# The norms' weights loaded with the first block of x, the first loads in order of use, and three constants made later

## The chip, the cores and the metric

The kernel runs on one core of a Trainium2 chip. The metric is the device time of one execution in microseconds (us). The core has TensorE (PE in the profile) for matmuls, VectorE (DVE), ScalarE (ACT) and GpSimd (POOL) for elementwise work, and SyncE (SP), which here only issues DMAs. SP, ScalarE and GpSimd each have a DMA queue of their own.

## The reference

The reference computes one step of a two-layer encoder for 256 prompt tokens and 32 sample tokens (288 columns), model width 1024, all in float32. Cut to what matters here:

```python
def rmsnorm(x, g):
    y = x * rsqrt(mean(x * x, axis=-1, keepdims=True) + 1e-6)
    return y * g

# layer 0 (layer 1 has another attention in the first two lines)
qa, ka, va, qb, kb, vb = proj_ab(rmsnorm(x, g_mix[0]), w_in_ab)
x = x + merge_heads(chunk_band_attn(qa, ka, va, rel_bias), stick_break_attn(qb, kb, vb)) @ w_out_ab
x = x + memory_attn(rmsnorm(x, g_xattn[0]), mem_k, mem_v)
x = x + swiglu(rmsnorm(x, g_ffn[0]))
# behind layer 1
y = rmsnorm(x, g_final)
```

There are nine norm weights g of 1024 numbers each (two layers of mix, xattn, mem and ffn, and the final one).

## The kernel before

Activations lie transposed: 8 blocks of 128 features by 288 tokens, block k in `x[k]`. Two blocks share a tile (`xh`, four tiles; L72, L73). The norm weights lie in a tile `gain` of 128 x 72 numbers, one column for each of the 9 norms and 8 blocks (L71).

Each weight matrix comes in units of 128 x 1024 floats: 8 blocks of 128 x 128, one for each block of features. float32 accuracy is had from three matmuls of a shorter type: a unit is split into a rounded part `hi` (a cast on ScalarE, L156) and the rest `lo` (a subtraction on VectorE, L157), the scaled activations likewise into `hh` (ScalarE, L291) and `hl` (VectorE, L294), and `mm3` (L183) issues hi x hh, hi x hl and lo x hh. The norm's row factor is applied after the projection; its sum of squares comes from `sq` (ScalarE, L243) and `ssq` (VectorE or GpSimd, L251), summed over features by the matmuls `nrm`.

**The start.** 32 small matmuls of an identity with itself (L134, `warm`) come first on TensorE; their sum is 32 times an identity. Then the first three projections (query, key and value of the first head pair) are computed side by side (`side_by_side`, L816): for each block k of x the three units' blocks, nine matmuls, 72 in all, and behind them the norm's sums `nrm`. The three units stand in a layout of their own, `w_first`: the 24 blocks in the order in which the matmuls use them, eight to a tile (`first`, three tiles), so block k of x uses blocks 3k to 3k+2. The casts of these tiles are cut into seven pieces (L1018): columns 0 to 384, 384 to 768 and 768 to 1024 of the first tile, halves of the other two. The loop at L1019 writes them between the splits of x's blocks.

**The loads** at the start (L84 to L92): on SP's queue the first 384 columns of the first weight tile, x's first tile (blocks 0 and 1), the gains, the rest of the first weight tile, the second weight tile, x's third tile and the third weight tile; on ScalarE's queue x's second and fourth tile. Behind them on SP come the units of the next projections (`st`, four buffers, shared with `first`).

**Constants.** `more_constants` (L140) is called at L1027, behind the loop. It makes on VectorE `ident` (the sum of the warming matmuls divided by 32), `fold` and `fold4` (sums of pieces of it) and `ntrir` (a copy of a triangular mask in the short type). `ident` is used first by the matmuls `nr` that spread the norm's row factor, and by all transposes; `fold` first by the sample tokens' attention, `fold4` by the gates of layer 1, `ntrir` by the stick-breaking heads.

**The order** on each engine is not the order of the code: a scheduler places the instructions, with the dependences that the code adds (`not_before`, L167). `behind` (L164) holds instructions of the first norm that the weight splits of the first heads must not pass.

**The first softmax** (`attend_prompt`, L406, and `softmax`, L386): scores `sc`; on VectorE the bias and maximum (L397); on ScalarE the exponentials `e` (L399); on VectorE reciprocals (L400) and the scaling of e (L402); on TensorE the transposes `tp` (L422 to L424); on ScalarE their copies `pt` (L428); on TensorE the products `po`.

Of the kernel before, what the change touches and what calls it, by code (L numbers as in the profile page):

```python
# [8 lines left out]
F32 = mybir.dt.float32  # L9
# [3 lines left out]
AF = mybir.ActivationFunctionType  # L13
ALU = mybir.AluOpType

P = 128
NT = 288
NP = 256
NS = 32
KT = 8  # L20
# [6 lines left out]
def encoder_step(ctx: ExitStack, tc: tile.TileContext, a):  # L27
# [6 lines left out]
    cst = ctx.enter_context(tc.tile_pool(name="cst", bufs=1))  # L34
    wp = ctx.enter_context(tc.tile_pool(name="wp", bufs=4))
    big = ctx.enter_context(tc.tile_pool(name="big", bufs=1))
# [5 lines left out]
    V, S, G, T, DMA = nc.vector, nc.scalar, nc.gpsimd, nc.tensor, nc.sync  # L42
# [25 lines left out]
        return T.matmul(out, lhsT, rhs, start=start, stop=stop, skip_group_check=True)  # L68


    gain = cst.tile([P, 9 * KT], F32, name="gain")  # L71
    xh = [big.tile([P, 2 * NT], F32, tag=f"x{i}", name=f"x{i}") for i in range(4)]  # L72
    x = [xh[k // 2][:, (k % 2) * NT:(k % 2) * NT + NT] for k in range(KT)]  # L73


    first = [wp.tile([P, 1024], F32, tag="st", bufs=4, name=f"first{i}") for i in range(3)]
# [1 line left out]
    def first_part(i, c0, c1):  # L78
        DMA.dma_start(first[i][:, c0:c1], a["w_first"][i][:, c0:c1])

    def x_part(i, eng=DMA):
        eng.dma_start(xh[i], a["xT"][:, 2 * i * NT:2 * (i + 1) * NT])

    first_part(0, 0, 384)  # L84
    x_part(0)
    x_part(1, S)
    x_part(3, S)
    DMA.dma_start(gain, a["gains"])
    first_part(0, 384, 1024)
    first_part(1, 0, 1024)  # L90
    x_part(2)
    first_part(2, 0, 1024)  # L92


    mean1 = cst.tile([P, 2], F32, name="mean1")
# [9 lines left out]
    ntri = cst.tile([P, P], F32, name="ntri")  # L105
    G.memset(ntri, -1.0)
    G.affine_select(out=ntri, in_=ntri, pattern=[[-1, P]], compare_op=ALU.is_ge, fill=0.0, base=0, channel_multiplier=1)
    ntrir = cst.tile([P, P], F32R, name="ntrir")
# [23 lines left out]
    warm = ps.tile([P, 512], F32, tag="at", bufs=4, name="warm")  # L132
    for i in range(32):
        warmed = T.matmul(warm[:, 0:P], identb, identb, start=i == 0, stop=i == 31)  # L134
    ident = cst.tile([P, P], F32, name="ident")
    fold = cst.tile([P, 2, 32], F32, name="fold")

    fold4 = cst.tile([P, 16], F32, name="fold4")

    def more_constants():  # L140
        V.tensor_scalar(ident, warm[:, 0:P], 1.0 / 32.0, None, op0=ALU.mult)
        by_head = ident.rearrange("p (j i q) -> p j i q", j=2, i=2)
        V.tensor_tensor(fold, by_head[:, :, 0], by_head[:, :, 1], ALU.add)
        V.tensor_tensor(fold4, fold[:, 0, 0:16], fold[:, 1, 0:16], ALU.add)
        V.tensor_copy(ntrir, ntri)

    wtab = cst.tile([P, 2], F32, name="wtab")
    S.activation(wtab, mean1, AF.Exp)
# [15 lines left out]
    began, behind, loads = [], [], []  # L164
# [620 lines left out]
    def evac_kv(cur, p, dst):  # L785
        t = tok("kv")

        def go():
            i = V.tensor_tensor(t, p[:, :NT], cur.r, ALU.mult)
            store(dst, t)  # L790
            return i

        cur.then(go)
        return t

    def rel_prompt(h):

        t = tok("bi")
        G.memset(t[64:128, 192:256], NEG)
        for p, n in ((0, 256), (64, 192)):  # L800
            G.dma_start(t[p:p + 64, 0:n], bass.AP(tensor=lined.tensor, offset=lined.offset + 384 * h + p + 1, ap=[[1, 64], [1, n]]))
        return t
# [6 lines left out]
    def mix_ab(cur, nxt, memory, w0):  # L809
        o = ([tok("oh", F32R) for _ in range(KT)], [tok("ol", F32R) for _ in range(KT)])  # L810
        qs, ks, vs, vns = {}, {}, {}, {}
        w = a["w_ab"]

        biases = {}

        def side_by_side():  # L816
            p = [att("pj"), acc("pj"), acc("pj")]
            with tc.issue_after(warmed.ins):
                for k in range(KT):
                    for u in range(3):  # L820
                        b = 3 * k + u
                        i = mm3(p[u][:, :NT], w0[b // 8], b % 8, cur.h, k, k == 0, k == KT - 1)
                        if k in (0, 5, 7) and u == 2:
                            began.append(i.ins)
            cur.y = cur.norm.columns()
            tick()
            return p

        def proj(j):
            hurry[0] = j < 4  # L830
            b = 12 * (j // 4) + j % 4
            kv = 8 * (j // 4) + j % 4
            p = side_by_side() if j == 0 else (project(w[b + 4 * i], cur.h) for i in range(3))
            p = iter(p)
            qs[j] = evac_q(cur, next(p), j < 4)
            ks[j] = evac_kv(cur, next(p), a["kv0"][kv])
            if j < 4:
                biases[j] = [rel_prompt(2 * j + i) for i in range(2)]
            vs[j] = evac_kv(cur, next(p), a["kv0"][kv + 4])

        def attention(j):
            args = (qs[j], ks[j], vs[j], vns, j)
            if j < 4:
                return attend_prompt(*args, biases.pop(j), o[0][j], o[1][j], (128, 0), True)
            return stick_prompt(*args, o[0][j], o[1][j])

        def attend(j):
            return later(attention(j), j == 0)

        def sample(g):  # L850
            two = (2 * g, 2 * g + 1)
            ck, cv = cached(g, lambda i: (a["cab"][2 * i], a["cab"][2 * i + 1]), 1 if g == 0 else 6)
            args = ([qs[j] for j in two], [ks[j] for j in two], two, vns, ck, cv)
            oo = ([o[0][j] for j in two], [o[1][j] for j in two])
            if g < 2:
                bias = rel_sample(g)
                yield 1
                yield from attend_sample(*args, bias, oo, True)
            else:
                yield from stick_sample(*args, oo)  # L860

        active.append(cur.scale())
        pairs(proj, attend, sample, memory, (0, 0, 0, 0, 2, 2, 2, 8))
        out_project(a["w_oab"], o, nxt, [6, 7])

# [158 lines left out]
            cur.norm.add(x[m - 2], V)  # L1024
    cur.norm.add(x[KT - 2], V)
    cur.norm.add(x[KT - 1], V)
    more_constants()  # L1027
    memories = [Memory(0), Memory(1)]
    for layer in range(2):
        nxt = Next(2 + layer)  # L1030
# [44 lines left out]
def _pack(inputs):  # L1075

    import numpy as np

    g = {k: np.asarray(v) for k, v in inputs.items()}

    def units(w):
        n = w.shape[1] // 128
        return w.reshape(8, 128, n, 128).transpose(2, 1, 0, 3).reshape(n, 128, 1024)

    def feats(t):
        n = t.shape[0]
        return t.T.reshape(8, 128, n).transpose(1, 0, 2).reshape(128, 8 * n)

    def keysT(c):
        n = c.shape[1] // 8  # L1090
        return c.reshape(128, n, 4, 128).transpose(1, 3, 2, 0).reshape(n, 128, 512)

    def vals(c):
        return c.reshape(128, -1, 512).transpose(1, 0, 2)

    x = np.concatenate([g["x_prompt"][0], g["x_sample"][0]], axis=0)
    gains = np.stack([g["g_mix"][0], g["g_mix"][1], g["g_xattn"][0], g["g_xattn"][1], g["g_mem"][0], g["g_mem"][1],
                      g["g_ffn"][0], g["g_ffn"][1], g["g_final"]])
    w_ab = units(g["w_in_ab"][0])
    w_g = np.pad(g["w_in_c"][0][:, 3072:], ((0, 0), (0, 16)))  # L1100
    cab = [keysT(g["cache_a_k"][0, 0])[0], vals(g["cache_a_v"][0, 0])[0],
           keysT(g["cache_b_k"][0, 0])[0], vals(g["cache_b_v"][0, 0])[0]]
    out = {
        "xT": feats(x), "memT": feats(g["mem_prompt"][0]),
        "gains": gains.reshape(9, 8, 128).transpose(2, 0, 1).reshape(128, 72),
        "w_ab": w_ab, "w_first": w_ab[[0, 4, 8]].reshape(3, 128, 8, 128).transpose(1, 2, 0, 3).reshape(128, 3, 1024).transpose(1, 0, 2), "w_oab": units(g["w_out_ab"][0]),
        "w_c": units(g["w_in_c"][0][:, :3072]), "w_g": w_g.reshape(8, 128, 32).transpose(1, 0, 2).reshape(128, 256), "w_oc": units(g["w_out_c"][0]),
        "w_xq": np.stack([units(w) for w in g["w_xq"]]), "w_xk": np.stack([units(w) for w in g["w_xk"]]),
        "w_xo": np.stack([units(w) for w in g["w_xo"]]),
        "w_xv": g["w_xv"].reshape(2, 2, 4, 128, 4, 256).transpose(0, 4, 1, 3, 2, 5).reshape(2, 4, 2, 128, 1024),  # L1110
        "w_gate": np.stack([units(w) for w in g["w_gate"]]), "w_up": np.stack([units(w) for w in g["w_up"]]),
        "w_down": g["w_down"].reshape(2, 22, 128, 8, 128).transpose(0, 2, 3, 1, 4).reshape(2, 128, 22, 1024).transpose(0, 2, 1, 3),
        "cab": np.stack(cab), "cck": keysT(g["cache_c_k"][0, 0]), "ccv": vals(g["cache_c_v"][0, 0]),
        "cmk": g["cache_mem_k"][:, 0].reshape(2, 256, 4, 2, 128).transpose(0, 2, 4, 3, 1).reshape(2, 4, 128, 512),
        "cmv": g["cache_mem_v"][:, 0].reshape(2, 2, 128, 4, 256).transpose(0, 3, 2, 1, 4).reshape(2, 4, 128, 512),
        "clf": g["cache_c_logf"][0, 0], "rel": g["rel_bias_a"][0].T[:, ::-1], "b_f": g["b_f_c"][0].reshape(16, 1),
    }
    return {k: np.ascontiguousarray(v) for k, v in out.items()}
# [29 lines left out]
```

## Time and profile before

| | us |
|---|---|
| median of 3 runs | 961.99 (961.39 to 962.18) |
| the profiled execution | 961.8 |
| its span, first to last instruction | 960.1 |
| TensorE busy | 946.0 (99%) |
| VectorE busy | 592.5 (62%) |
| ScalarE busy | 484.3 (50%) |
| mean granted TensorE clock | 0.998 |

A row of the timeline has start and duration in us, the engine, the line of the kernel, the operation, the tiles written and read without their numbers, the shapes, the count, and in brackets how long the engine sat idle before it and what ended that. An engine's name with a q (SPq) is its instruction queue, where DMAs are issued. In the stretches each engine's busy time stands with its instruction count in brackets. Starts of a pipelined engine may lie closer together than a duration, so what an instruction costs in a row of others is read from start to start.

### The profile page before, as it was taken

The page shows a single profiled execution, that of the slowest core. Times are in us where ns is not written, and L with a number is a line of the kernel's source. Part 1 is how long each engine was busy: PE and PEld are TensorE (multiplying, and loading weights), DVE is VectorE, ACT ScalarE, POOL GpSimd, SP SyncE. Part 2 cuts the span into 40 slices and gives each one's busy share as a digit, 9 for nine tenths or more (in the row PEclk, how much of TensorE's full clock was granted, in tenths as well). Part 3 has the DMA queues.
Part 4 walks back from the last instruction along what each step waited for, and adds up shares of the span by engine and source line. Part 5 has one row for each costly group of instructions (what it writes and reads, how often), then busy time and mean ns, then how long its engine had stood idle before and what let it go on. Part 6 is the DMA issues. An engine that isn't in the chain of part 4 may idle for free.

```text
span 960.1 us, 19047 instructions
## 1 busy us (share of the span) xinstructions
PE 946.0 (99%) x7476; PEld 912.3 (95%) x7476; DVE 592.5 (62%) x1137; ACT 484.3 (50%) x860; POOL 239.3 (25%) x358
## 2 busy tenths in 40 slices
PE   8999999999999999999999999999999999999997
PEld 7889999999999999999999999999989999999996
DVE  6786556676765555855466666667658555555452
ACT  5566777544554444444346454455446544444331
POOL 4341123400222222410125432532012222222010
PEclk9999999999999999999999999999999999999999
DMA  7665446544344444454455454545425444444431
GB/s 274 195 211 198 156 167 184 189 154 130 120 158 160 171 172 158 175 199 175 168 207 188 165 201 165 182 153 189 158 79 176 155 174 162 169 167 163 175 111 50
DMA packets 49258, 160.97 MB, mean 168 GB/s; under 512 B 7304, under 2 KB 8136, under 8 KB 49168
## 3 DMA queue, kind: packets, MB, share of 16 engines
q1 hardware_dynamic: 44976, 149.12, 45.3%
q0 software_dynamic: 3904, 10.04, 3.0%
q8 instruction: 59, 0.97, 0.4%
q10 hardware_dynamic: 288, 0.59, 0.2%
q14 instruction: 31, 0.25, 0.1%
HBM read 149.58 MB, written 10.15 MB: 166 GB/s over the span
## 4 chain that ended last, share of the span: by engine, by line
PE 92%; DVE 3%; ACT 2%; DMA 1%; issue 1%; POOL 0%; DVEq 0%; SPq 0%; ACTq 0%; POOLq 0%
PE pj L68 52%; PE dn L68 15%; PE op L68 10%; PE mv L68 5%; PE po L68 1%; PE xo L68 1%; PE zb L68 1%; PE xs L68 1%; PE sc L68 1%; DVE lo L157 1%; DMA st<-w_ab 1%; ACT hi L156 1%; PE nrm L68 1%; ACT e L399 1%; PE xss L68 1%
## 5 line engine op out<-in xcount | busy, mean ns | idle before, releaser
L156 ACT CAST hi<-st 128x1024 fp32r<-128x1024 f32 x257 | 269.5, 1050 | 320.4 <-issue 128.0
L68 PE MATMUL pj<-hh,hi 128*128 128x288 f32 (+1 forms) x1344 | 399.8, 298 | 1.1 <-ACT hh L291 1.1
L68 PE MATMUL pj<-hh,lo 128*128 128x288 f32 (+1 forms) x1344 | 395.8, 294 | 0.0
L68 PE MATMUL pj<-hl,hi 128*128 128x288 f32 (+1 forms) x1344 | 394.2, 293 | 0.5 <-DVE hl L294 0.5
L157 DVE TENSOR_TENSOR lo<-st,hi 128x1024 fp32r<-128x1024 f32 x257 | 320.7, 1248 | 97.5 <-PE dn L68 42.7
L68 PEld LDWEIGHTS pj<-hh,hi 128*128 128x128 f32 x1344 | 253.0, 188 | 8.5 <-issue 5.7
L68 PEld LDWEIGHTS pj<-hl,hi 128*128 128x128 f32 x1344 | 253.1, 188 | 0.9 <-DVE hl L294 0.9
L68 PEld LDWEIGHTS pj<-hh,lo 128*128 128x128 f32 x1344 | 252.5, 188 | 0.2 <-DVE lo L157 0.2
L68 PE MATMUL dn<-fh,hi 128*128 128x288 f32 x400 | 108.8, 295 | 0.0
L68 PE MATMUL dn<-fh,lo 128*128 128x288 f32 x352 | 103.8, 295 | 0.0
L68 PE MATMUL dn<-fl,hi 128*128 128x288 f32 x304 | 89.5, 294 | 0.0
L68 PE MATMUL op<-ol,hi 128*128 128x288 f32 x256 | 75.7, 296 | 0.0
L68 PE MATMUL op<-oh,hi 128*128 128x288 f32 x256 | 75.7, 298 | 0.0
L68 PE MATMUL op<-oh,lo 128*128 128x288 f32 x256 | 75.3, 295 | 0.0
L68 PEld LDWEIGHTS dn<-fh,hi 128*128 128x128 f32 x400 | 72.6, 188 | 0.0
L68 PEld LDWEIGHTS dn<-fh,lo 128*128 128x128 f32 x352 | 66.2, 188 | 0.0
L251 POOL TENSOR_TENSOR ssq<-ssq,sq 128x288 f32<-128x288 f32 (+1 forms) x35 | 36.4, 1041 | 114.7 <-ACT sq L243 70.8
L754 POOL TENSOR_TENSOR fl<-us,fh 128x288 fp32r<-128x288 f32 x38 | 33.8, 890 | 120.0 <-ACT fh L753 120.0
L749 DVE TENSOR_TENSOR us<-pj,rstd 128x288 f32<-128x288 f32 x44 | 20.1, 458 | 60.8 <-PE pj L68 60.8
L750 POOL TENSOR_TENSOR gs<-gs,sg 128x288 f32<-128x288 f32 x44 | 38.8, 883 | 74.3 <-ACT sg L748 72.8
L68 PEld LDWEIGHTS dn<-fl,hi 128*128 128x128 f32 x304 | 57.2, 188 | 0.0
L68 PEld LDWEIGHTS op<-ol,hi 128*128 128x128 f32 x256 | 48.2, 188 | 0.6 <-issue 0.4
(268 smaller groups left out, 1260.8 us busy)
## 6 DMA issues: line engine op xcount, KB each, us to landing
st<-w_gate SPq DMA_DIRECT2D x44, 512.0 KB, 3.5
st<-w_up SPq DMA_DIRECT2D x44, 512.0 KB, 3.2
st<-w_down SPq DMA_DIRECT2D x44, 512.0 KB, 3.2
st<-w_c SPq DMA_DIRECT2D x24, 512.0 KB, 3.3
st<-w_ab SPq DMA_DIRECT2D x21, 512.0 KB, 4.7
st<-w_xk SPq DMA_DIRECT2D x16, 512.0 KB, 4.0
st<-w_xv SPq DMA_DIRECT2D x16, 512.0 KB, 3.5
st<-w_xq SPq DMA_DIRECT2D x16, 512.0 KB, 3.4
```

Of the source, the lines that this page charges most:

```text
L68: return T.matmul(out, lhsT, rhs, start=start, stop=stop, skip_group_check=True)
L156: a = S.copy(hi, st[:, c0:c1])
L157: b = V.tensor_tensor(lo, st[:, c0:c1], hi.bitcast(F32), ALU.subtract)
L251: eng.tensor_tensor(s[:, :self.n], self.acc[i][:, :self.n], q[:, :self.n], ALU.add)
L399: S.activation(out[:, c0:c1], out[:, c0:c1], AF.Exp, bias=mx, scale=-1.0, accum_out=sm)
L749: V.tensor_tensor(us, pu[:, :NT], cur.r, ALU.mult)
L750: G.tensor_tensor(gs, gs, sg, ALU.mult)
L754: G.tensor_tensor(lo, us, hi.bitcast(F32), ALU.subtract)
```

## The change

The gains are no longer a tensor of their own: they are laid in front of x in the input `xT`, and x's first tile becomes 72 columns wider to hold them. On ScalarE's queue the first load is now the gains with block 0, then x's second tile. On SP's queue: 384 columns of the first weight tile, block 1 by itself, the rest of the first weight tile, x's third tile, the second weight tile, half of the third, x's fourth tile, the other half. `ident` is made by ScalarE behind the loop; `fold`, `fold4` and `ntrir` are made by VectorE after the key projection of the third head pair in the code, not before the last instruction in `behind`.

```diff
-    gain = cst.tile([P, 9 * KT], F32, name="gain")
-    xh = [big.tile([P, 2 * NT], F32, tag=f"x{i}", name=f"x{i}") for i in range(4)]
-    x = [xh[k // 2][:, (k % 2) * NT:(k % 2) * NT + NT] for k in range(KT)]
+    G0 = 9 * KT
+    xh = [big.tile([P, 2 * NT + (0 if i else G0)], F32, tag=f"x{i}", name=f"x{i}") for i in range(4)]
+    gain = xh[0][:, 0:G0]
+    x = [xh[k // 2][:, (0 if k > 1 else G0) + (k % 2) * NT:][:, :NT] for k in range(KT)]
...
-    def x_part(i, eng=DMA):
-        eng.dma_start(xh[i], a["xT"][:, 2 * i * NT:2 * (i + 1) * NT])
-
+    def x_part(i):
+        DMA.dma_start(xh[i], a["xT"][:, G0 + 2 * i * NT:G0 + 2 * (i + 1) * NT])
+
+    S.dma_start(xh[0][:, 0:G0 + NT], a["xT"][:, 0:G0 + NT])
+    S.dma_start(xh[1], a["xT"][:, G0 + 2 * NT:G0 + 4 * NT])
     first_part(0, 0, 384)
-    x_part(0)
-    x_part(1, S)
-    x_part(3, S)
-    DMA.dma_start(gain, a["gains"])
+    DMA.dma_start(x[1], a["xT"][:, G0 + NT:G0 + 2 * NT])
     first_part(0, 384, 1024)
+    x_part(2)
     first_part(1, 0, 1024)
-    x_part(2)
-    first_part(2, 0, 1024)
+    first_part(2, 0, 512)
+    x_part(3)
+    first_part(2, 512, 1024)
...
     def more_constants():
-        V.tensor_scalar(ident, warm[:, 0:P], 1.0 / 32.0, None, op0=ALU.mult)
         by_head = ident.rearrange("p (j i q) -> p j i q", j=2, i=2)
-        V.tensor_tensor(fold, by_head[:, :, 0], by_head[:, :, 1], ALU.add)
-        V.tensor_tensor(fold4, fold[:, 0, 0:16], fold[:, 1, 0:16], ALU.add)
-        V.tensor_copy(ntrir, ntri)
+        for i in (V.tensor_tensor(fold, by_head[:, :, 0], by_head[:, :, 1], ALU.add),
+                  V.tensor_tensor(fold4, fold[:, 0, 0:16], fold[:, 1, 0:16], ALU.add),
+                  V.tensor_copy(ntrir, ntri)):
+            not_before(i, behind[-1])
...
             if j < 4:
                 biases[j] = [rel_prompt(2 * j + i) for i in range(2)]
+            if j == 2:
+                more_constants()
             vs[j] = evac_kv(cur, next(p), a["kv0"][kv + 4])
...
     cur.norm.add(x[KT - 1], V)
-    more_constants()
+    S.activation(ident, warm[:, 0:P], AF.Copy, scale=1.0 / 32.0)
```

The scheduler moves more than the code does. ScalarE at the start, from its first work on data to the second half of the second weight tile, before (`first_83` to `first_85` are the three weight tiles, `x_79` to `x_82` the four tiles of x):

```order
L156 CAST hi_177<-first_83 128x384
L291 ACTIVATE hh_183<-x_79,gain 128x288
L291 ACTIVATE hh_189<-x_79,gain 128x288
L156 CAST hi_177<-first_83 128x384
L291 ACTIVATE hh_195<-x_80,gain 128x288
L156 CAST hi_177<-first_83 128x256
L243 ACTIVATE sq_203<-x_79 128x288
L291 ACTIVATE hh_205<-x_80,gain 128x288
L156 CAST hi_179<-first_84 128x512
L243 ACTIVATE sq_209<-x_79 128x288
L156 CAST hi_179<-first_84 128x512
L291 ACTIVATE hh_213<-x_81,gain 128x288
```

And now (numbers one lower, `x_78` the first tile of x with the gains in it):

```order
L294 ACTIVATE hh_183<-x_78 128x288
L159 CAST hi_177<-first_82 128x384
L294 ACTIVATE hh_189<-x_78 128x288
L159 CAST hi_177<-first_82 128x384
L294 ACTIVATE hh_195<-x_79,x_78 128x288
L159 CAST hi_177<-first_82 128x256
L246 ACTIVATE sq_203<-x_78 128x288
L294 ACTIVATE hh_205<-x_79,x_78 128x288
L246 ACTIVATE sq_209<-x_78 128x288
L159 CAST hi_179<-first_83 128x512
L294 ACTIVATE hh_213<-x_80,x_78 128x288
L159 CAST hi_179<-first_83 128x512
```

Block 0's hh now stands ahead of the first weight cast, block 1's square ahead of the first cast of the second weight tile, and the hh of block 4 between that tile's two casts.

VectorE at the first softmax of the first head pair, from the low part of a weight unit to the next values, before (`e_468` and `e_480` are the two heads):

```order
L157 TENSOR_TENSOR lo_626<-st_623,hi_625 128x1024
L400 RECIPROCAL st_469<-st_469 128x2
L402 TENSOR_SCALAR e_468<-e_468,st_469 128x128
L402 TENSOR_SCALAR e_468<-e_468,st_469 128x256
L400 RECIPROCAL st_481<-st_481 128x2
L402 TENSOR_SCALAR e_480<-e_480,st_481 128x128
L402 TENSOR_SCALAR e_480<-e_480,st_481 128x256
L789 TENSOR_TENSOR kv_543<-pj_506,rstd_418 128x288
```

And now (`e_465` and `e_477` are the same two heads):

```order
L160 TENSOR_TENSOR lo_623<-st_620,hi_622 128x1024
L403 RECIPROCAL st_466<-st_466 128x2
L145 TENSOR_TENSOR fold<-ident 128x64
L405 TENSOR_SCALAR e_465<-e_465,st_466 128x128
L405 TENSOR_SCALAR e_465<-e_465,st_466 128x256
L403 RECIPROCAL st_478<-st_478 128x2
L146 TENSOR_TENSOR fold_167<-fold 128x16
L147 CAST ntrir<-ntri 128x128
L405 TENSOR_SCALAR e_477<-e_477,st_478 128x128
L405 TENSOR_SCALAR e_477<-e_477,st_478 128x256
L792 TENSOR_TENSOR kv_540<-pj_503,rstd_415 128x288
```

The three constants stand behind the two reciprocals, ahead of the scaling of each head's e.

ScalarE at the same softmax, before (`pt` are the copies of the transposed e of the two heads, `st_700` a weight unit):

```order
L399 ACTIVATE e_480,st_481<-e_480,st_481 128x256
L428 COPY pt_535<-tp_531 128x384
L156 CAST hi_702<-st_700 128x1024
L428 COPY pt_541<-tp_537 128x384
L373 CAST oh_263<-po_577 128x256
```

And now:

```order
L402 ACTIVATE e_477,st_478<-e_477,st_478 128x256
L159 CAST hi_702<-st_700 128x1024
L431 COPY pt_532<-tp_528 128x384
L431 COPY pt_538<-tp_534 128x384
L376 CAST oh_260<-po_574 128x256
```

The weight cast has moved ahead of both copies. On TensorE the only change of order is at these transposes: the first matmul of the next projection, which stood behind the second head's first transpose, now stands ahead of it, the second ahead of its other two. GpSimd's order is unchanged.

More of the change, by code (lines that the diff above doesn't have):

```diff
@@ L1098, in _pack @@
                       g["g_ffn"][0], g["g_ffn"][1], g["g_final"]])
+    gains = gains.reshape(9, 8, 128).transpose(2, 0, 1).reshape(128, 72)
     w_ab = units(g["w_in_ab"][0])
@@ L1103, in _pack @@
     out = {
-        "xT": feats(x), "memT": feats(g["mem_prompt"][0]),
-        "gains": gains.reshape(9, 8, 128).transpose(2, 0, 1).reshape(128, 72),
+        "xT": np.concatenate([gains, feats(x)], axis=1), "memT": feats(g["mem_prompt"][0]),
         "w_ab": w_ab, "w_first": w_ab[[0, 4, 8]].reshape(3, 128, 8, 128).transpose(1, 2, 0, 3).reshape(128, 3, 1024).transpose(1, 0, 2), "w_oab": units(g["w_out_ab"][0]),
```

## The prediction

> **What bounds the kernel now.** I read the page first, then the busy time by stretches, then the timelines of TensorE, ScalarE and VectorE in the first 36 us, where the change acts.
>
> ```profile
> span 960.1 us, 19047 instructions
> PE 946.0 (99%) x7476; PEld 912.3 (95%) x7476; DVE 592.5 (62%) x1137; ACT 484.3 (50%) x860; POOL 239.3 (25%) x358
> ```
>
> The stretches (busy time and number of instructions of each engine, granted clock, share of the DMA engines, GB/s):
>
> ```profile
> 0.00:8.00 8.00, 4.16 (x34) 3.69 (x35) 1.30 (x3) 3.31 (x7) 4.43 (x26) 1.00 0.76 260
> 8.00:16.00 8.00, 7.69 (x57) 7.45 (x58) 7.85 (x21) 8.00 (x21) 5.37 (x13) 1.00 0.90 314
> 100.00:960.10 860.10, 851.30 (x6710) 826.58 (x6708) 520.79 (x945) 423.25 (x728) 205.56 (x280) 1.00 0.47 162
> ```
>
> From 100 us on, TensorE is idle for 8.8 of 860 us: whatever the start saves moves everything behind it forward by the same amount and no more. Only the first stretch leaves TensorE empty. In the second ScalarE has no idle time at all and VectorE 0.15 us. So the question is by how much the 72 matmuls of the first three projections end earlier. TensorE there (start, duration):
>
> ```profile
> 2.57 3.60 PE L134 MATMUL warm<-identb 128*128 128x128 bf16 x32 [2.57 <-POOL identb masks.py:199]
> 7.28 0.40 PE L68 MATMUL pj<-hh,hi 128*128 128x288 f32 x1 [1.12 <-ACT hh L291]
> 7.83 0.40 PE L68 MATMUL pj<-hl,hi 128*128 128x288 f32 x1 [0.15 <-DVE hl L294]
> 8.20 0.30 PE L68 MATMUL pj<-hh,hi 128*128 128x288 f32 x1
> ...
> 13.79 0.29 PE L68 MATMUL pj<-hh,hi 128*128 128x288 f32 x1
> 14.40 0.40 PE L68 MATMUL pj<-hl,hi 128*128 128x288 f32 x1 [0.31 <-DVE hl L294]
> ...
> 17.80 0.29 PE L68 MATMUL pj<-hh,lo 128*128 128x288 f32 x1
> 17.93 0.80 PE L68 MATMUL nrm<-mean,ssq 128*128 128x2 f32 x6
> ```
>
> The row at 8.20 is the 4th of the 72 and the one at 13.79 the 46th: 42 steps in 5.59 us, 0.133 us each. 72 of them need 9.58 us. The warming matmuls end at 2.57 + 3.60 = 6.17, and the norm's sums start at 17.93, 11.76 us later. TensorE therefore loses 11.76 - 9.58 = 2.18 us in this stage, at its start and at 13.79. **2.18 us is the most that the change can win here**, since it leaves the warming matmuls alone.
>
> What starts it late is ScalarE's wait:
>
> ```profile
> 4.60 0.51 ACT L156 CAST hi<-first 128x384 fp32r<-128x384 f32 x1 [1.36 <-DMA first<-w_first]
> 6.69 0.96 ACT L291 ACTIVATE hh<-x,gain 128x288 fp32r<-128x288 f32 x2 [1.58 <-DMA gain<-gains]
> 7.56 0.49 ACT L156 CAST hi<-first 128x384 fp32r<-128x384 f32 x1
> ...
> 9.47 0.60 ACT L156 CAST hi<-first 128x512 fp32r<-128x512 f32 x1
> 9.98 0.44 ACT L243 ACTIVATE sq<-x 128x288 f32<-128x288 f32 x1
> 10.33 0.61 ACT L156 CAST hi<-first 128x512 fp32r<-128x512 f32 x1
> ```
>
> After its first cast ScalarE waits 1.58 us for the 36 KB of gains, third on SP's queue, and then has work without a break.
>
> **The change, part by part.** *Gains with x's first block.* The first transfer on ScalarE's queue now carries gains and block 0 together (128 x 360 floats, 0.184 MB) and is the first there, as today's first weights (released at 4.60) are on SP's. So I let the first hh start at about 4.5, the cast of the first weights at 4.9 and block 1's hh at 5.3; all three are done before TensorE leaves its warming at 6.17. The 1.58 us wait for the gains goes. What is late next is the second piece of the first weights (columns 384 to 1024): blocks 3 to 7 of the 24 lie in it.
>
> *The order of the loads.* That piece has 1.15 MB to share the engines with: on SP's queue 0.197 + 0.147 + 0.328, on ScalarE's 0.184 + 0.295. Today the gains had, by the same count, 0.197 + 0.295 + 0.037 on SP's and 0.295 + 0.295 on ScalarE's, 1.12 MB, and were released at 6.69. The DMA answers for 2 to 6 and for 6 to 12 us say how fast that goes:
>
> ```profile
> DMA packets 789, 1.24 MB, mean 309 GB/s; under 512 B 228, under 2 KB 358, under 8 KB 789
> ```
> ```profile
> DMA packets 813, 2.51 MB, mean 419 GB/s; under 512 B 108, under 2 KB 116, under 8 KB 813
> ```
>
> Late end: the same release as the gains plus 0.03 MB at 419 GB/s, 6.69 + 0.08, about 6.75. Early end: 1.15 MB have moved by 5.8, and half a microsecond (my estimate) from last byte to first instruction, 6.3. I take 6.5, between them: ScalarE casts this piece 1.06 us earlier than at 7.56, not 1.58 + something.
>
> From that cast to the first cast of the second weight tile ScalarE takes 9.47 - 7.56 = 1.91 us today. The new order puts one more square ahead of it (the order of x's blocks is changed), 10.33 - 9.98 = 0.35, so 2.26: it comes at 8.76 (8.56 to 9.01). The second tile's bytes don't bind: 1.97 MB must have moved, 1.24 by 6.0 and 0.73 more at 419 GB/s, 7.75. VectorE then makes the low part:
>
> ```profile
> 10.11 0.69 DVE L157 TENSOR_TENSOR lo<-first,hi 128x512 fp32r<-128x512 f32 x1
> 12.12 0.22 DVE L145 CAST ntrir<-ntri 128x128 fp32r<-128x128 f32 x1
> 13.82 0.52 DVE L294 SCALAR_TENSOR_TENSOR hl<-x,gain,hh 128x288 fp32r<-128x288 f32 x1
> 14.62 0.29 DVE L141 TENSOR_SCALAR ident<-warm 128x128 f32<-128x128 f32 x1
> 15.25 0.22 DVE L143 TENSOR_TENSOR fold<-ident 128x64 f32<-128x64 f32 x1
> 15.75 0.17 DVE L144 TENSOR_TENSOR fold<-fold 128x16 f32<-128x16 f32 x1
> ```
>
> It ends at 10.11 + 0.69 = 10.80 today, 1.33 us after the cast's start; so at 10.09 then (9.9 to 10.35). It is the 27th matmul that needs it. Without waits the 27th would start at 6.2 + 26 x 0.133 = 9.66, so TensorE waits there for some 0.45 us, and the other 45 follow: 10.1 + 45 x 0.133 = 16.1, and the norm's sums at 16.25 (16.05 to 16.5). Against 17.93 that is **1.7 us (1.4 to 1.9)**.
>
> *VectorE's constants.* The copy ntrir (0.22) stood before the low part that delayed the hl of 13.82, for which TensorE waited until 14.40. It, ident (0.29), fold (0.22) and fold4 (0.17) leave this stage: at most 0.90 us off VectorE. With the new order hl comes ahead of the second half's low part, so that wait should vanish; it is inside the 1.7. Ident becomes a ScalarE instruction, between squares, ahead of the last hh. I price it at 0.29, as on VectorE, at most the 0.44 of a square; TensorE needs the last hh only for its last nine matmuls, so it is covered.
>
> The three others return in the first softmax, between the reciprocals and the scaling of e, just before TensorE's transposes:
>
> ```profile
> 30.57 0.16 DVE L400 RECIPROCAL st<-st 128x2 f32<-128x2 f32 x1
> 30.76 0.55 DVE L402 TENSOR_SCALAR e<-e,st 128x128 f32<-128x128 f32 x2
> ```
> ```profile
> 30.38 0.29 PE L68 MATMUL pj<-hh,lo 128*128 128x288 f32 x1
> ...
> 30.71 0.33 PE L423 MATMUL tp<-ident,e 128*128 128x128 f32 x1
> ...
> 31.20 0.30 PE L422 MATMUL tp<-ident,e 128*128 128x128 f32 x1
> ...
> 34.83 0.88 PE L68 MATMUL po<-pt,vn 128*64 128x256 f32 x8
> ```
>
> The transpose at 31.20 waits for e already, so a delay shows on TensorE: at most 0.22 + 0.17 + 0.22 = 0.61, at least nothing (they fit the time in which e waits for its reciprocal, 30.57 to 30.76). Against it stands one projection matmul, 0.133, which now fills that wait. I take 0.1 lost, nearer to nothing since today's gap after a reciprocal holds an instruction.
>
> **The sum**: 1.7 - 0.1 = 1.6 us. The profiled execution took 961.8 (span 960.1 and 1.7 around it), the median of the runs is 961.99; 0.2 us between them. On the median: **960.4 us**, its own range 960.1 to 961.0. What this measurement can tell from no change is 0.2%, 1.92 us, so the forecast reads as "the same" although I expect a real gain.
>
> A rule against the change: it makes ten first loads of nine, two of them halves of what was one. The DMA rows above show 419 GB/s with such loads queued behind each other. The Trainium skill (DMA: Bandwidth & Descriptors, Rules for kernel authors and Anatomy of one DMA) wants small transfers coalesced and gives each about 2.0 us of fixed cost, by which one more would make it 962.4 (an estimate); the trace does not agree that this adds up, since 2.51 MB passed in those 6 us.
>
> **The rivals.** *TensorE never waits* (0.26). If the second piece lands early and VectorE, rid of its constants, keeps up, the cap is reached: 2.18 less 0.1, 2.1 us, 959.9, faster by over 0.2%. For it: VectorE had 0.15 us idle in 8 us and loses up to 0.90 of work. Against it: ScalarE's own chain to 8.56 at the earliest.
>
> *TensorE starts too early for its clock* (0.12). The 32 warming matmuls took 3.60 / 32 = 0.1125 us for 128 columns, later ones 0.133 for 288; at the warming pace 288 columns would take 0.253 (an estimate, other types), 0.12 more each. Now the projection starts directly at 6.2, not at 7.28. The wait at the 27th hides 0.45, four matmuls; ten slow ones cost 1.2 - 0.45 = 0.75: gain 0.85, 961.1. Against it: the granted clock reads 1.00 in the first stretch. The Trainium skill (TensorE: Matmul & The Clock Gate, Part 1) has TensorE at half clock until a window of some 3.4 us was busy, with a phase that varies by run; no row here shows the phase.
>
> *One more transfer costs its own price* (0.04). The first weight piece was released 4.60 - 0.82 = 3.8 us after SP began to issue; if a tenth load had to pay half of that by itself, 1.9 us, the gain is gone: 1.6 - 1.9, or 0.3 slower, 962.3. Against it speaks that the loads overlap in the rows above. The row of SP's issue:
>
> ```profile
> 0.82 0.39 SPq L79 DMA_DIRECT2D first<-w_first  x1
> ```
>
> *Slower* (0.07). ScalarE's order also changes at the first softmax: a cast of 1024 columns, behind a weight load, now stands ahead of both copies of the transposed weights pt, which TensorE needs at 34.83:
>
> ```profile
> 31.18 0.48 ACT L428 COPY pt<-tp 128x384 f32<-128x384 f32 x1 [1.32 <-PE tp L424]
> 31.56 1.05 ACT L156 CAST hi<-st 128x1024 fp32r<-128x1024 f32 x1
> 32.51 0.48 ACT L428 COPY pt<-tp 128x384 f32<-128x384 f32 x1
> ```
> ```profile
> 26.01 0.33 SPq L178 DMA_DIRECT2D st<-w_ab  x1
> ```
> ```profile
> 58.56 6.35 DMA st<-w_ab
> ```
>
> If that load, issued at 26.01, lands at t, the copies end at t + 1.05 + 0.38 + 0.48 and TensorE is held once t is over 32.9, a load of 6.9 us. The slowest on the chain took 6.35. To end 2.0 us slower it must hold TensorE 3.6 us, a load of 10.5 us, behind the bias rows which GpSimd loads at the same time: 964.0. Little speaks for it.
>
> **How the numbers follow.** Forecast 0.51 at 960.4; never waits 0.26 at 959.9; clock 0.12 at 961.1; own price 0.04 at 962.3; slower 0.07 at 964.0. Faster is the second and a fifth of the first's early end (0.06): 0.32. Slower 0.07. Same 0.61. For 8 in 10 the range takes the first three cases, with their bounds: 959.4, a little below the cap for waits that vanish later by chance, to 961.9.
>
> **What would show it.** Right: the first hh near 4.5 with no wait for gains; the first projection matmul at 6.2; a wait of about 0.45 us at the 27th on the low part; the norm's sums near 16.25; the second pair of transposes at most 0.2 us later against the matmul before them. Wrong: the cast of the second piece later than 6.75 or earlier than 6.3, projection matmuls further apart than 0.133 behind 6.2, or a start moved by 1.6 us and an end not moved with it.

## The result and the profile after

The changed kernel is slower: 963.96 us (963.40 to 964.39, 15 runs) against 961.91 us (961.34 to 962.38, 15 runs), a ratio of 1.0020 [1.0013, 1.0028]. The forecast was 960.4, and 963.96 lies above its range. The profiled execution took 964.12 us (span 962.4), 2.3 more than the one before.

The start itself went as forecast. ScalarE in the kernel after, in the order of its work:

```profile
4.65 0.53 ACT L294 ACTIVATE hh<-x 128x288 fp32r<-128x288 f32 x1 [1.41 <-DMA x<-xT]
5.09 0.49 ACT L159 CAST hi<-first 128x384 fp32r<-128x384 f32 x1
5.51 0.53 ACT L294 ACTIVATE hh<-x 128x288 fp32r<-128x288 f32 x1
6.55 0.51 ACT L159 CAST hi<-first 128x384 fp32r<-128x384 f32 x1 [0.50 <-DMA first<-w_first]
...
8.81 0.60 ACT L159 CAST hi<-first 128x512 fp32r<-128x512 f32 x1
```

VectorE's low part of the second tile:

```profile
9.45 0.69 DVE L160 TENSOR_TENSOR lo<-first,hi 128x512 fp32r<-128x512 f32 x1
```

And TensorE:

```profile
5.92 0.59 PE L68 MATMUL pj<-hh,hi 128*128 128x288 f32 x1
6.31 0.44 PE L68 MATMUL pj<-hl,hi 128*128 128x288 f32 x1
6.55 0.44 PE L68 MATMUL pj<-hh,lo 128*128 128x288 f32 x1
6.79 0.35 PE L68 MATMUL pj<-hh,hi 128*128 128x288 f32 x1
...
9.78 0.29 PE L68 MATMUL pj<-hl,hi 128*128 128x288 f32 x1
10.20 0.40 PE L68 MATMUL pj<-hh,lo 128*128 128x288 f32 x1
...
16.40 0.74 PE L68 MATMUL nrm<-mean,ssq 128*128 128x2 f32 x6
```

The wait for the gains is gone, the second piece's cast stands at 6.55, the 27th matmul at 10.20 is the only one that waits, and the norm's sums start at 16.40, not 17.93: 1.53 us are won.

They are lost again later, and at no single place. The sums `nrm` occur in the same places of TensorE's order in every kernel of this study, so they serve as marks: from the second group (the memory's norm) to the first group of the final norm TensorE has 6829 instructions. Before:

```profile
79.89 0.51 PE L68 MATMUL nrm<-mean,ssq 128*128 128x2 f32 x4
...
949.17 0.73 PE L68 MATMUL nrm<-mean,ssq 128*128 128x2 f32 x6
```

After:

```profile
78.51 0.51 PE L68 MATMUL nrm<-mean,ssq 128*128 128x2 f32 x4
...
951.37 0.73 PE L68 MATMUL nrm<-mean,ssq 128*128 128x2 f32 x6
```

The lead is 1.38 us at the first mark, and at the second the kernel after is 2.20 late. Between them it takes 872.86 us, the kernel before 869.28: **3.58 us more for the same instructions**. A wait would show as idle time. The stretches say there is none, before (134 us in the gate and up projections of the first layer; the number in brackets behind an engine's busy time counts its instructions, TensorE first):

```profile
276.00:410.00 134.00, 134.00 (x1018) 134.00 (x1017) 83.75 (x123) 63.48 (x88) 41.22 (x43) 1.00 0.49 169
```

and after:

```profile
100.00:960.10 860.10, 853.56 (x6699) 828.92 (x6697) 518.91 (x944) 422.01 (x723) 205.01 (x279) 1.00 0.47 161
276.00:410.00 134.00, 134.00 (x1012) 134.00 (x1011) 82.43 (x123) 62.91 (x87) 41.44 (x43) 1.00 0.50 170
```

TensorE is busy for the whole of the 134 us in both, at a granted clock of 1.00 in both, and does six matmuls fewer after. From 100 us on it is even busier than before (853.56 against 851.30 us) and does less (6699 instructions against 6710). The step from one start to the next, over consecutive matmuls of the projections `pj`, `dn` and `op` (288 columns, a few of 256) from 100 us on and with steps of 150 ns or more left out, is 131.46 ns before (mean of 5226 steps of the trace) and 132.17 ns after (5218 steps): a matmul became 0.7 ns, half a per cent, slower on average. Of the 3.58 us, 3.45 are in these three projections.

What can do this to matmuls that the change doesn't touch? It also moves tiles in SBUF, the core's memory for tiles; places here are bytes from the start of a partition. The gains' tile of 288 bytes per partition stood in front of all constants and weight tiles, so that without it the weight tiles (`first` and `st`, `hi`, `lo`) start 288 bytes lower. x's first tile lies behind them and is 288 bytes larger, so that `hh`, `hl` and all that follows stay. Before, `hi` starts at byte 41472 and the tiles of h at 89856, both multiples of 128; after, `hi` starts at 41184, 96 past a multiple of 128. In the matmuls of the projections a block of `hi` or `lo` is the weights, and `hh` or `hl` is the moving operand, whose columns pass through them one after the other.

### The profile page after: what moved, and what is told of

Its sections match the earlier page's. It is cut to its first block, busy times and chain, and to the rows that moved or that the text cites. A ratio compares the mean times of both kernels' runs of the same rounds, so it can differ in the third digit from the quotient of the medians.

```text
span 962.4 us, 19052 instructions
## 1 busy us (share of the span) xinstructions
PE 949.8 (99%) x7476; PEld 916.5 (95%) x7476; DVE 590.7 (61%) x1136; ACT 484.5 (50%) x861; POOL 239.7 (25%) x358
## 4 chain that ended last, share of the span: by engine, by line
PE 93%; DVE 3%; ACT 2%; DMA 1%; issue 1%; POOL 0%; DVEq 0%; SPq 0%; ACTq 0%; POOLq 0%
PE pj L68 53%; PE dn L68 15%; PE op L68 10%; PE mv L68 5%; PE po L68 1%; PE xo L68 1%; PE zb L68 1%; PE xs L68 1%; PE sc L68 1%; DMA st<-w_ab 1%; DVE lo L160 1%; PE nrm L68 1%; ACT e L402 1%; PE xss L68 1%; ACT hi L159 1%
```

## The experiments

In the first four expectations, A is the theory that the tiles' places cost the time; B and C put it down to the new order of loads and instructions. From the fifth on, A says that a tile has to start at a multiple of 128 bytes, B that the distance between the weight tiles and the tiles of h counts. All the results stand in one table at the end of this section.

**The change's layout without the change.** The gains' tile goes to the pool behind the weights. Instructions and loads are those of the kernel before, the places those of the kernel after:

```diff
-    gain = cst.tile([P, 9 * KT], F32, name="gain")
+    gain = big.tile([P, 9 * KT], F32, tag="gain", name="gain")
```

> The kernel before, with its own order and loads, and only the tile of the gains placed behind the weights in memory, so that constants and weight tiles start 288 bytes lower, exactly where the changed kernel has them. Theory A: slower by the 3.6 us that the changed kernel lost behind its start, 965.5 us, with matmuls 0.1328 us apart. Theory B: no change, 961.9 us. Theory C (x's block 0, which alone also lies off, is the cause): no change either, since x stays where it was.

Measured: 965.99 us (965.98 to 966.41), ratio 1.0042 [1.0029, 1.0054]. Its marks:

```profile
80.39 0.51 PE L68 MATMUL nrm<-mean,ssq 128*128 128x2 f32 x4
...
953.17 0.73 PE L68 MATMUL nrm<-mean,ssq 128*128 128x2 f32 x6
```

872.78 us between them, as in the kernel after (872.86). No load and no instruction was changed: the places alone make the loss.

**The change without its layout.** 32 unused bytes in front and a wider first tile of x put the weights of the kernel after back on multiples of 128:

```diff
+    cst.tile([P, 8], F32, name="pad")
-    xh = [big.tile([P, 2 * NT + (0 if i else G0)], F32, tag=f"x{i}", name=f"x{i}") for i in range(4)]
+    xh = [big.tile([P, 2 * NT + (0 if i else 96)], F32, tag=f"x{i}", name=f"x{i}") for i in range(4)]
```

> The changed kernel with 32 bytes of padding ahead of the constants and x's first tile widened by 96 bytes: every weight tile starts at a multiple of 128 bytes again, as in the kernel before, and no instruction differs. Theory A (the weights' addresses slow every matmul): the norm's sums stay at 16.4 us and the matmuls of the large stages go back from 0.1328 to 0.1320 us each, so the start's 1.5 us is kept to the end: 960.4 us. Theory B (the new order of loads and instructions itself costs time later): no change, 964.0 us.

Measured: 961.14 us (960.83 to 961.45), ratio 0.9989 [0.9980, 0.9998], and 870.48 us between the marks: most of the loss is gone, but 1.2 us of it stay, which alignment to 128 bytes doesn't explain.

**Which tiles.** Unused bytes around the split weights, so that of the weights only `hi` and `lo` move to 32 past a multiple of 128, or only the loaded `st`; the 96 bytes behind fill up to 128, so that all that follows stands 128 higher:

```diff
+    wp.tile([P, 8], F32, tag="pad", bufs=1, name="pad")
     w0 = [unit_tiles() for _ in first]
+    wp.tile([P, 24], F32, tag="pad2", bufs=1, name="pad2")
```

> The kernel before with 32 bytes of padding between the tiles that the weights are loaded into and the tiles of their hi and lo parts, and 96 bytes behind these: only hi and lo start at 32 past a multiple of 128. Theory A, in the form that the matmuls' weight loads read across a line: all of the loss, 965.5 us. In the form that the DMA writes of the loaded weights are what costs: no change, 961.9 us.

```diff
+    wp.tile([P, 8], F32, tag="pad", bufs=1, name="pad")
     first = [wp.tile([P, 1024], F32, tag="st", bufs=4, name=f"first{i}") for i in range(3)]
...
+    wp.tile([P, 24], F32, tag="pad2", bufs=1, name="pad2")
     w0 = [unit_tiles() for _ in first]
```

> The kernel before with 32 bytes of padding ahead of the tiles that the weights are loaded into and 96 bytes behind them: only the loaded float32 weights start at 32 past a multiple of 128, hi and lo where they were modulo 128. If TensorE's own reads are what slows it: no change, 961.9 us. If the DMA's writes (or the reads by ScalarE and VectorE) collide with the matmuls: all of the loss, 965.5 us.

Measured: 964.46 us (963.72 to 965.73), ratio 1.0025 [1.0016, 1.0035], with `hi` and `lo` moved; 962.58 (961.69 to 963.63), 1.0004 [0.9995, 1.0013], with `st` moved. Moving what DMAs write, and ScalarE and VectorE read, by 32 bytes costs nothing clear of the noise. Moving what TensorE reads costs 2.3 us between the marks, not the whole 3.6 that the first form of its expectation had.

**Alignment or distance.** First a kernel after that leaves everything behind x's tiles just where the kernel before has it, the weights 1152 bytes higher:

```diff
-    xh = [big.tile([P, 2 * NT + (0 if i else G0)], F32, tag=f"x{i}", name=f"x{i}") for i in range(4)]
-    gain = xh[0][:, 0:G0]
+    x0 = cst.tile([P, G0 + NT], F32, name="x0")
+    xh = [big.tile([P, (2 if i else 1) * NT], F32, tag=f"x{i}", name=f"x{i}") for i in range(4)]
+    gain = x0[:, 0:G0]
...
-    S.dma_start(xh[0][:, 0:G0 + NT], a["xT"][:, 0:G0 + NT])
+    S.dma_start(x0, a["xT"][:, 0:G0 + NT])
```

> The kernel after with the gains and x's first block in a tile of their own, 1440 bytes, which lies where the gains' tile lay in the kernel before. The weight tiles so start 1152 bytes (9 x 128) above their places in the kernel before, and all that lies behind x's tiles stands just where it stood before. Theory A (the weight tiles' alignment to 128 bytes sets the step of every matmul): the start's 1.5 us stay, 960.5 +- 0.5. Rival B (any move of the weight tiles against the tiles of h costs, aligned or not): the later part loses 1 to 3 us, 962 to 964.

Then the kernel before, with unused bytes behind x's tiles (32 columns of 4 bytes; 8 columns in the second), and with the places of the realigned kernel after:

```diff
+    big.tile([P, 32], F32, tag="pad", name="pad")
     w0 = [unit_tiles() for _ in first]
```

> The kernel before with 128 unused bytes behind x's tiles: the weight tiles stay, and the tiles of h, of the softmax and of the norms all start 128 bytes higher. The alignment of both stays, their distance changes by 128. Theory A (alignment alone): as before, 961.9 +- 0.4. Rival B (the distance between the two operands): a change of up to 2 us either way, seen evenly in all projections.

> The kernel before with 32 unused bytes behind x's tiles: the weight tiles stay at multiples of 128 bytes, the tiles of h and everything behind them start at 32 past one. Theory A1 (what counts is that a tile read by TensorE starts on a line, moving operand as well as weights): about 2 to 3.5 us slower, 964 to 965.5. Theory A2 (the weights' reads alone): 961.9 +- 0.4. Rival B (the distance of the two): no size of its own, up to 2 us either way.

```diff
-    gain = cst.tile([P, 9 * KT], F32, name="gain")
+    cst.tile([P, 8], F32, name="pad")
+    gain = big.tile([P, 9 * KT + 24], F32, tag="gain", name="gain")[:, 0:9 * KT]
```

> The kernel before, its instructions and loads unchanged, with the addresses of the realigned kernel after (weights 256 bytes lower than before, tiles of h 128 higher; both at multiples of 128). That one gave back 1 us of its lead between 69 and 929 us. If the layout does that (rival B, distance): 962.9 +- 0.5, the loss in the later part again about 1 us. If the aligned layout is free (theory A) and the 1 us came with the new order of loads: 961.9 +- 0.4.

Measured: 961.20, 963.57, 965.64 and 963.55 us. The second and the fourth lose 1.6 us with the weights and h at multiples of 128: alignment alone can't be it. Between the marks the first, second and fourth take 870.5 to 870.6, as the realigned kernel after did; in all four the distance between the weight tiles and h is 128 bytes more than before, modulo 256. The third, with the weights untouched and h moved by 32, takes 872.83: as the kernel after, whose distance is also 32 more. The decisive kernel is then one in which all tiles are off the multiples of 128 and the distance is the old one; the gains' tile 32 bytes larger does that:

```diff
-    gain = cst.tile([P, 9 * KT], F32, name="gain")
+    gain = cst.tile([P, 9 * KT + 8], F32, name="gain")[:, 0:9 * KT]
```

> The kernel before with the gains' tile 32 bytes larger, so that the weight tiles, x, h and all that follows start 32 bytes higher together: weights and h both at 32 past a multiple of 128, as the kernel after's weights are, but at the same distance from each other as in the kernel before. Alignment (theory A): both operands are off the line, 965.6 or more. Distance (theory B, now the likelier: the kernels that keep the distance modulo 256 bytes keep the step of 131.5 ns, those with 32 more or less modulo 256 have 132.1 to 132.2, with 128 131.7): 961.9 +- 0.4, and a mean step as in the kernel before.

Measured: 962.38 us (961.74 to 963.64), ratio 0.9999 [0.9990, 1.0008]; between the marks 869.47:

```profile
81.37 0.51 PE L68 MATMUL nrm<-mean,ssq 128*128 128x2 f32 x4
...
950.84 0.73 PE L68 MATMUL nrm<-mean,ssq 128*128 128x2 f32 x6
```

Its step is 131.46 ns, that of the kernel before. What counts is the distance.

**The change with the old distance, and its two halves.** The kernel after with the gains' 288 bytes left empty in front, and x's first tile 512 bytes wider than in the kernel before:

```diff
+    cst.tile([P, G0], F32, name="pad")
-    xh = [big.tile([P, 2 * NT + (0 if i else G0)], F32, tag=f"x{i}", name=f"x{i}") for i in range(4)]
+    xh = [big.tile([P, 2 * NT + (0 if i else 128)], F32, tag=f"x{i}", name=f"x{i}") for i in range(4)]
```

> The kernel after, its instructions and loads unchanged, with an unused tile of 288 bytes where the gains' tile was, and x's first tile 512 bytes wider than in the kernel before: the weight tiles stand where they stood before, h and the rest 512 bytes higher, so the distance is the same modulo 256 (and 512). Theory B: the step of the kernel before comes back and the start's 1.5 us are kept: 960.4 +- 0.4. Should the distance count modulo 1024 or more: between 960.4 and 963.

Measured: 959.67 us (959.37 to 959.85), ratio 0.9972 [0.9960, 0.9983]. The marks:

```profile
77.71 0.51 PE L68 MATMUL nrm<-mean,ssq 128*128 128x2 f32 x4
...
947.12 0.73 PE L68 MATMUL nrm<-mean,ssq 128*128 128x2 f32 x6
```

2.18 us ahead of the kernel before at the first and 2.05 at the second, so that the lead is now kept between the marks. Not all of it comes from the start, though: at 66 us this kernel leads by 1.42, and the other 0.7 come from a wait at the second softmax, which the next experiment takes up.

From this kernel, the constants put back (the edit of `more_constants`, its call and `ident` undone), and to the kernel before the constants' part of the diff alone:

> The kernel after with the kept distance, and VectorE's constants where the kernel before has them (all four operations of VectorE right behind the norm's squares): the loads alone. The constants stood in the prediction at 0.1 us or less beside the first softmax, and the norm at the start waits for lo and not for them: within 0.3 us of the same kernel with the constants moved, 960.5 +- 0.5. If the constants carry a part of the start's gain, up to 0.6 us above it.

> The kernel before with the constants of the kernel after (identity on ScalarE, the three others behind the first norm) and nothing else; every tile where it was. The norm's sums start at 17.93 us because the last lo is late, which the constants do not touch: 961.9 +- 0.4. If they hold VectorE at the start: 961.3 or less.

Measured: the loads alone 960.27 us (959.71 to 960.42), ratio 0.9978 [0.9969, 0.9988]; the constants alone 961.29 (960.62 to 962.39), 0.9991 [0.9982, 1.0]. The loads win 1.8 us of 962.08. The constants win 0.6 on top of them, and between nothing and 1.7 by themselves; both expectations had this as their second case. The traces show where. With the loads alone the norm's sums at the start wait for VectorE:

```profile
16.90 0.83 PE L68 MATMUL nrm<-mean,ssq 128*128 128x2 f32 x6 [0.21 <-DVE ssq L255]
```

With the constants moved as well they don't:

```profile
16.60 0.72 PE L68 MATMUL nrm<-mean,ssq 128*128 128x2 f32 x6
```

VectorE, without the constants, begins the low part behind the squares at 16.27 instead of 16.76 us, and the same 0.49 us lie between the two kernels at the first mark (77.71 and 78.20). So the constants did hold VectorE at the start.

A wait further on looks like their work too and isn't. TensorE in the second softmax, in the kernel before:

```profile
68.91 0.30 PE L422 MATMUL tp<-ident,e 128*128 128x128 f32 x1 [0.27 <-DVE e L402]
69.63 0.33 PE L423 MATMUL tp<-ident,e 128*128 128x128 f32 x1 [0.41 <-DVE e L402]
```

and with the constants alone moved:

```profile
67.79 0.30 PE L422 MATMUL tp<-ident,e 128*128 128x128 f32 x1
68.43 0.33 PE L423 MATMUL tp<-ident,e 128*128 128x128 f32 x1 [0.35 <-DVE e L402]
```

One of two waits for VectorE is gone, and 0.7 us with it. But from the projection matmul at 66.32 to the one at 71.47 the kernels before and after take 5.1 to 5.2 us and all sixteen others 4.4 to 4.8, among them the loads alone and nine kernels with the instructions and loads of the kernel before. So neither the loads nor the constants decide it. What does stays open.

**Period and grain of the distance.** The kernel before with 16, then 64 unused columns behind x's tiles, in the place of the 32 above:

> The kernel before with 64 unused bytes behind x's tiles: the distance between the weight tiles and h changes by 64. Theory B holds that the distance sets the step, with its own value for each remainder: a change by 32 cost 3.6 us, by 128 cost 1.6 us. If the step goes by whether the two fall on the same 128-byte line position, 64 costs as 32 does: 965.5 +- 0.6. If it goes by 64-byte pieces: as 128 or as none, 962 to 963.7.

> The kernel before with 256 unused bytes behind x's tiles: the distance changes by 256. If it counts modulo 256: 961.9 +- 0.4 and the step of the kernel before in each of pj, dn and op. If it counts modulo 512 or more: another step, 1 to 3 us slower; the kernel after with 512 bytes more between them, which had the old step, would not contradict that.

Measured: 960.95 us (959.74 to 962.74), ratio 0.9986 [0.9978, 0.9994], for 64; 961.66 (961.42 to 963.52), 0.9993 [0.9985, 1.0002], for 256. 256 is as nothing; 64 is faster than what the kernel before has, which neither form of its expectation allowed. So the kernel after was tried with these: the one with the old distance, x's first tile wider by 144 columns than two blocks instead of 128, and by 176:

> The kernel after with its weight tiles where they stood before and the tiles of h 576 bytes higher (64 modulo 256): the start of the kernel after and the distance that made the kernel before 1.1 us faster. If the two add up, as theory B has it: 959.67 - 1.06, 958.6 +- 0.5. If the gain of the distance was the other kernels' noise: 959.7.

> The same with 704 bytes (192 modulo 256). The tiles of h are 1152 bytes apart, so that half of them stand 128 further, modulo 256, than the others: 64 and 192 only swap the halves. 958.6 +- 0.6 if the halves count alike; up to 1.5 us more if not, as 0 and 128 differ by 1.6.

Measured: 958.82 us (958.35 to 958.98), ratio 0.9964 [0.9952, 0.9977], the fastest of the study; and 959.45 (959.03 to 959.78), 0.9972 [0.9962, 0.9983].

Most of what 64 wins isn't in the projections counted so far. Of its 1.78 us between the marks 1.4 are in the 384 matmuls `mv` (the memory's values), in which the roles are swapped: `hi` and `lo` are the moving operand, the tiles of h the weights. The mean step of `mv` is 118.8 ns in the kernel before, 114.5 with h up 64, and 114.1 and 115.0 in the last two kernels. The step of `pj`, `dn` and `op` is 131.33 ns with h up 64, but 131.56 and 131.64 in the last two, more than the 131.46 of the kernel before. The sum came out as expected for 576, not matmul by matmul.

**All of them.** The shift is that of h against `hi` and `lo`, compared with the kernel before, modulo 256 bytes. The next columns are the place of `hi` modulo 128, the median and its ratio to the kernel before, and the time between the two marks in the profiled execution.

| kernel | shift | `hi` mod 128 | median us | ratio | between the marks |
|---|---|---|---|---|---|
| before | 0 | 0 | 961.91 to 962.27 | | 869.28 |
| before, st moved | 0 | 0 | 962.58 | 1.0004 | 869.54 |
| before, all up 32 | 0 | 32 | 962.38 | 0.9999 | 869.47 |
| before, h up 256 | 0 | 0 | 961.66 | 0.9993 | 869.43 |
| before, constants alone | 0 | 0 | 961.29 | 0.9991 | 869.42 |
| after, loads alone, h up 512 | 0 | 0 | 960.27 | 0.9978 | 869.47 |
| after, h up 512 | 0 | 0 | 959.67 | 0.9972 | 869.41 |
| **after** | 32 | 96 | 963.96 | 1.0020 | 872.86 |
| before, gains moved | 32 | 96 | 965.99 | 1.0042 | 872.78 |
| before, h up 32 | 32 | 0 | 965.64 | 1.0043 | 872.83 |
| before, hi and lo moved | 96 | 32 | 964.46 | 1.0025 | 871.59 |
| before, h up 128 | 128 | 0 | 963.57 | 1.0018 | 870.57 |
| before, layout of the realigned | 128 | 0 | 963.55 | 1.0016 | 870.51 |
| after, realigned | 128 | 0 | 961.14 | 0.9989 | 870.48 |
| after, weights up 1152 | 128 | 0 | 961.20 | 0.9992 | 870.54 |
| before, h up 64 | 64 | 0 | 960.95 | 0.9986 | 867.50 |
| after, h up 576 | 64 | 0 | 958.82 | 0.9964 | 868.29 |
| after, h up 704 | 192 | 0 | 959.45 | 0.9972 | 868.97 |

The last column goes by the shift: seven kernels at 869.3 to 869.5, three at 872.8 to 872.9, four at 870.5 to 870.6, whatever their loads, their order or the place of `hi`. What stays open: why the distance counts, since the profile has no row for a read of SBUF; its full period, since 0, 256 and 512 are alike but 64 and 576 differ by 0.8 us; and 96, for which there is one kernel alone.

## Why the prediction was wrong, point by point

- **The step that failed** is the sentence under the stretches: "whatever the start saves moves everything behind it forward by the same amount and no more". It took the pace of the other 7400 matmuls as given because no instruction of theirs changes. Between the marks they take 3.58 us more, and 1.38 of lead less 3.58 is the 2.20 by which the final norm is late. With the distance kept the sentence holds between the marks, to 0.13 us (2.18 ahead at the first, 2.05 at the second). The prediction's last sign of being wrong, a start moved and an end not moved with it, is what came.
- **The start, 1.7 us (1.4 to 1.9):** right. First hh 4.5, measured 4.65; the second piece's cast 6.5, measured 6.55; the second tile's 8.76, measured 8.81; the end of its low part 10.09, measured 9.45 + 0.69 = 10.14; the norm's sums 16.25, measured 16.40, 1.53 us ahead. The half microsecond from last byte to first instruction was 0.40 for the second piece (its last packet ended at 6.15). Loads and constants share this win: with the loads alone the sums start at 16.90, 1.03 us ahead. The wait at the 27th was 0.45 and came to 10.20 - 9.78 - 0.13 = 0.29, since the matmuls ahead of it ran later.
- **The constants, 0.1 lost:** right for the place it was meant for. The kernel after is 1.61 us ahead just before the first softmax (28.64 against 30.25) and 1.52 behind it (31.50 against 33.02); with the constants alone nothing is lost there (0.42 ahead before it, 0.47 behind). That VectorE is rid of them at the start was counted inside the 1.7; as a whole they win 0.6 us beside the loads (959.67 against 960.27).
- **TensorE never waits:** no, the 27th waits, for ScalarE's chain as argued against it.
- **TensorE starts too early for its clock:** its mechanism is there. The steps from 6.31 to 6.79 take 0.24 us each, and full pace is reached behind them. Those few slow steps fall into the wait at the 27th, as forecast; other executions have more of them (below). The granted clock of 1.00 in the first stretch, held against this rival, was no evidence: the warming matmuls of that stretch start 0.107 us apart, and 0.056 in the kernel with `st` moved once its clock record says full, at 5.33 us.
- **One more transfer costs its own price:** no, the second piece came within 0.05 of the time worked out from the bytes.
- **Slower, by a ScalarE cast ahead of the copies of pt:** no, the lead is 1.52 us behind that softmax and 1.38 still at 78.51. The kernel is slower for a reason that none of the rivals named: the layout of SBUF, which the diff changes in its very first line.

## What to carry to other kernels

Taking out, adding or resizing a tile is a change to every tile behind it in SBUF: write down where the operands of the busiest engine lie before and after, and put unused bytes in the place of what was taken out, so that a new order of work is timed in the old layout. Where an engine is busy for 99% of the time, a mark that occurs in both traces at the same instruction number tells a slower pace from a wait; the share of busy time doesn't. And once the pace is known to depend on the layout, a few distances are worth a try: 64 bytes were worth 1.1 us to the kernel before, loads and constants with the old distance 2.4.

## What the runs showed of the hardware

- A matmul's step depends on the distance in SBUF between its weights and its moving operand. For `pj`, `dn` and `op` the means from 100 us on are 131.46 ns at a shift of 0, 131.33 at 64 (131.56 at 576), 131.68 at 128, 131.93 at 96 and 132.13 at 32, at a granted clock of 1.00; for `mv` 118.8 at 0 and 114.5 at 64. With all tiles 32 bytes higher together the step stays 131.46.
- How long TensorE runs at about half pace at the start differs between executions of the same instructions. The kernel with all tiles 32 bytes higher has the same order and loads as the kernel before; its stretch from 8 to 16 us and its first steps:

```profile
8.00:16.00 8.00, 8.00 (x40) 7.87 (x40) 7.93 (x20) 8.00 (x21) 5.20 (x13) 1.00 0.90 316
```

```profile
8.54 0.44 PE L68 MATMUL pj<-hh,lo 128*128 128x288 f32 x1
8.78 0.44 PE L68 MATMUL pj<-hh,hi 128*128 128x288 f32 x1
9.02 0.44 PE L68 MATMUL pj<-hl,hi 128*128 128x288 f32 x1
```

  It does 40 instructions where the kernel before does 57, with steps of 0.24 us until 14.0, and its norm's sums start at 20.29, not 17.93. The column of the granted clock reads 1.00 in both. It counts the time ahead of the first record of the clock as full, and that record is at 6.46 us in the kernel before and at 14.09 in this one. Where the clock was full before it fell, the column shows the fall. The kernel with `st` moved, whose steps are 0.13 us until 8.7 and 0.24 from 8.9 to 12.0:

```profile
9.00:12.00 3.00, 3.00 (x14) 3.00 (x14) 2.86 (x7) 3.00 (x8) 0.79 (x3) 0.50 1.01 395
```

  The Trainium skill (TensorE: Matmul & The Clock Gate, Part 1) has a half clock that ends with a window of 3.4 us which runs freely and not from the kernel's start. The traces agree: in this kernel the clock is full from 5.33 us, half from 8.74 and full from 12.15, changes that lie 3.41 us apart, and the times differ from one execution to the next.
- In the eleven profiled kernels with the old order of loads TensorE idles for 1.1 to 1.7 us behind the warming matmuls. Five of them have the norm's sums at 17.9 to 18.1 us, and six, whose clock is at half until 11.2 to 14.1 us, at 18.9 to 20.4. In the seven with the new order it goes from the one to the other without idling, the clock is full from 6.2 to 8.3 us on, and the sums start at 16.3 to 16.9. So the new order also spares the late starts; what that adds to the medians is not known, since each kernel has one trace.
